# Three tiles of a depthwise convolution on TensorE with four taps stacked on partitions

## The chip, the core and the metric

The kernel runs on one core of a Trainium2 chip. The metric is the device time of one execution in microseconds; the time before is the median of three runs. A core has four engines that compute, each with an instruction stream of its own that it works through in order: TensorE (PE, matmuls), VectorE (DVE), ScalarE (ACT) and GpSimd (POOL). DMAs are issued from SP or from one of the other streams. What one engine needs of another it waits for on a semaphore.

## The reference

The program is two transformer blocks for 256 tokens of 1024 channels. The first block has two layers, each with a feed-forward part before and after its mixer; the mixer of the first layer is the convolution module that the change touches:

```python
def conv_module(h, w_pw1, w_dw, g_norm, w_pw2):
    u = h @ w_pw1
    a, b = jnp.split(u, 2, axis=-1)
    u = a * jax.nn.sigmoid(b)
    u = lax.conv_general_dilated(u, w_dw[:, None, :], window_strides=(1,),
        padding=[(CONV_WIDTH - 1, 0)], dimension_numbers=("NWC", "WIO", "NWC"),
        feature_group_count=D_MODEL)
    u = jax.nn.silu(rmsnorm(u, g_norm))
    return u @ w_pw2
```

CONV_WIDTH is 31, so every channel is its own causal filter of 31 taps over the tokens. Work of the second block that needs nothing of the first (the projections of its context tokens with `w_in_2`, gates, scans and states) is done early, beside the convolution.

## The kernel before

Channels lie on partitions: 1024 channels are 8 tiles of 128, tokens along the free axis. `conv` (L632) runs in about 210 to 385 us of the span. In a loop over four pairs of tiles it takes two parts of `conv_w_pw1`, projects (`proj_pair`), multiplies one half by the sigmoid of the other (L655 to L658) and leaves two tiles of `up`, 31 columns wider than the tokens. Weights come as 1 MB loads `raw` on SP; each part is split into a high piece `whi` on ScalarE (L193) and the rest `wlo` on VectorE (L197), and the projection takes three matmuls (L301 to L303) for each product.

The 31 taps of a tile are done in one of three ways:
- `taps` (L695) on VectorE: 31 instructions, the first L701, the others L703, each adding one shifted copy of `up` times a channel's weight into `cv`. Tiles 2, 3, 5, 6.
- `taps_pool` (L708): ScalarE makes four products at a time (L717, tile `taps`, two buffers), GpSimd sums them (L711). Tiles 0, 1, 4.
- `taps_pe` (L727) on TensorE: ScalarE scales the identity into 31 diagonal matrices (L736), TensorE adds 31 matmuls into one PSUM tile `ctaps` (L741, L744), ScalarE copies it out and squares it. Tile 7 (CONV_PE, at the end of the class).

These three are generators. `tick` (L353) takes pieces of the waiting ones while other code is written out: in the projections four pieces of VectorE's lane and one of GpSimd's per weight part (CONV_RATE = 4, 1), later sixteen and three per step (CONV_RATE2) of the loop that writes out the context's work (`fill` until "late"). That work is `cp` on TensorE in blocks of 16 matmuls (two records of the profile each; L1135, L1139), the sigmoids `sg` on ScalarE, gates `cfk` and scans on VectorE, the keys' norm (`ks`, `rsm` to `rx`, `krb`, `dup`), then transposes `ctr` and the state's matmuls `cs`. The order in which code is written out is the order of each engine's stream; nothing is moved afterwards.

At the end, `rstd_from_sum` takes the sums of squares of all tiles (`vsvector`, `vsgpsimd`), VectorE makes the scale (`rsm` to `dg`), TensorE broadcasts it (`rb`, L426), and the scaled result (L435) goes into the output projection `pd`.

Of the kernel before, what the change touches and what calls it, by code (L numbers as in the profile page):

```python
# [8 lines left out]
F32 = mybir.dt.float32  # L9
# [3 lines left out]
AF = mybir.ActivationFunctionType  # L13
ALU = mybir.AluOpType
# [3 lines left out]
P = 128  # L18
T = 256
D = 1024  # L20
KD = 8
# [20 lines left out]
def hmask(p):  # L42

    s, c = p[:, None] % 32, np.arange(32)[None, :]
    lv = []
    for b in (1, 2, 4, 8, 16):
        same = s // (2 * b) == c // (2 * b)
        lv.append(same & (s // b < c // b))
        lv.append(same & (s // b > c // b))
    return np.concatenate(lv, 1).astype(np.float32)  # L50


def constants():

    p = np.arange(P)
    f32 = np.float32
    parts = {}
    parts["ident"] = np.eye(P, dtype=f32)
    parts["ones"] = np.ones((P, P), f32)
    parts["iota_p"] = np.stack([p, p + P], 1).astype(f32)  # L60
    parts["other"] = (p[:, None] // 32 != np.arange(4)[None, :]).astype(f32) * 1024
    rot = np.zeros((P, P), f32)
    for m in range(P):
        b, r = divmod(m, 64)
        if r < 32:
            rot[b * 64 + r + 32, m] = -1.0
        else:
            rot[b * 64 + r - 32, m] = 1.0
    parts["rot"] = rot
    rot = np.zeros((P, P), f32)  # L70
    for m in range(P):
        b, r = divmod(m, 32)
        if r < 16:
            rot[b * 32 + r + 16, m] = -1.0
        else:
            rot[b * 32 + r - 16, m] = 1.0
    parts["rot_ax"] = rot
    for i in range(2):
        sel = np.zeros((P, P), f32)
        for m in range(P):  # L80
            sel[i * 64 + m % 64, m] = 1.0
        parts[f"dup{i}"] = sel
    parts["blk64"] = (p[:, None] // 64 == p[None, :] // 64).astype(f32)
    t = np.arange(T)
    ang = np.zeros((P, T), f32)
    for q in range(P):
        r = q % 64
        ang[q] = (t // 64 if r < 32 else t % 64).astype(f32) * INV_FREQ_AX[r % 16]
    parts["cos_ax"] = np.cos(ang.astype(np.float64)).astype(f32)
    parts["sin_ax"] = np.sin(ang.astype(np.float64)).astype(f32)  # L90
    parts["invf"] = INV_FREQ[p % 32][:, None]
    parts["hmask"] = hmask(p)
    parts["iota_t"] = np.broadcast_to(t.astype(f32), (P, T)).copy()
    cols, off = {}, 0
    for n, a in parts.items():
        cols[n] = (off, a.shape[1])
        off += a.shape[1]
    return np.ascontiguousarray(np.concatenate(list(parts.values()), 1)), cols


CONST, CCOL = constants()
N_IDENT = CCOL["rot"][0]
N_EARLY = CCOL["iota_t"][0]
# [158 lines left out]
def wcols(name, idx, c0, n, k0=0, nk=None):  # L262

    def load(A, eng, v):
        w = A[name]
        for i in idx:
            w = w[i]
        if len(w.shape) == 3:
            w = w.rearrange("c h d -> c (h d)")
        w = w.rearrange("(k p) f -> p k f", p=P)  # L270
        eng.dma_start(v, w[:, k0:k0 + nk, c0:c0 + n])
    return load
# [12 lines left out]
def two(a):  # L285

    return a.rearrange("p (a t) -> p a t", a=2)


class Kernel:  # L290
# [341 lines left out]
    def conv(self, x, sums, done, sp):  # L632
        nc = self.nc
        late = self.late_rb(sums)
        with self.tc.tile_pool(name="conv", bufs=1) as cp:
            up = cp.tile([P, KD, T + 32], F32, name="up")
            nc.gpsimd.memset(up[:, :, 0:32], 0.0)
            v = cp.tile([P, KD, T], F32, name="cv")

            self.vs = {n: cp.tile([P, T], F32, name="vs" + n) for n in ("vector", "gpsimd")}  # L640
            self.vs_used = []
            self.fillers += [self.context(cp, sp), self.adaln(1)]
            self.rate = self.CONV_RATE
            pe = []
            for c in range(4):
                w = self.S.get(KD, 256, wcols("conv_w_pw1", (0,), 1024 + 256 * c, 256, 0, KD))
                pb = self.proj_pair(w, x, KD)
                if c == 0:
                    next(late)
                w = self.S.get(KD, 256, wcols("conv_w_pw1", (0,), 256 * c, 256, 0, KD))  # L650
                pa = self.proj_pair(w, x, KD)
                if c == 0:
                    rb = next(late)
                sb = self.tmp.tile([P, 512], F32, name="sg", tag="sg")
                nc.vector.tensor_tensor(two(sb), two(pb), rb, op=ALU.mult)  # L655
                nc.scalar.activation(sb, sb, AF.Sigmoid)
                nc.vector.tensor_tensor(two(sb), two(sb), rb, op=ALU.mult)
                nc.vector.tensor_tensor(up[:, 2 * c:2 * c + 2, 32:], pa.rearrange("p (a t) -> p a t", a=2),  # L658
                                        sb.rearrange("p (a t) -> p a t", a=2), op=ALU.mult)
                for k in (2 * c, 2 * c + 1):  # L660
                    if k in self.CONV_PE:
                        pe.append(self.taps_pe(cp, v[:, k], up[:, k], k))
                    elif k in self.CONV_POOL:
                        self.background[1].append(self.taps_pool(cp, v[:, k], up[:, k], k))
                    else:
                        self.background[0].append(self.taps(v[:, k], up[:, k], k))
            pe = chain(*pe)
            while self.fill(1) != "late":
                self.tick(self.CONV_RATE2)
                next(pe, None)  # L670
            self.rate = 0, 0
            for _ in pe:
                pass
            self.tick_all()
            self.warm(AF.Sqrt)
            r = self.rstd_from_sum(self.tok_sums([self.vs[n] for n in self.vs_used]), D)
            w = self.S.ahead(2)
            dg = self.diag(r)
            self.fill(self.CONV_FILL[0])
            self.warm(AF.Silu)  # L680
            rb = self.bcast(r, dg)
            for low, eng in zip(w, (nc.vector, nc.gpsimd)):
                low(eng)
            self.S.n_hl = 2
            y = (sp.tile([P, KD, T], F32R, name="yh", tag="hc"), cp.tile([P, KD, T], F32R, name="yl", tag="cb"))
            b = cp.tile([P, 4, T], F32, name="taps", tag="taps", bufs=2)
            xn = cycle([b[:, i] for i in range(4)])
            self.apply_norm(v, rb, lambda k: self.V("conv_norm", k), y[0], y[1], KD, AF.Silu,
                            new=lambda: next(xn))
            self.fill(self.CONV_FILL[1])  # L690
            self.S.n_hl = self.N_HL
            return self.out_proj(y, KD, self.by_k("conv_w_pw2"), done(1.0, (self.CONV_FILL[2],) * 8),
                                 self.WIDE[0])
# [30 lines left out]
        self.add_sq_on("gpsimd", acc, pool.tile([P, 4, T], F32, name="taps", tag="taps", bufs=2)[:, 0])  # L724
        yield

    def taps_pe(self, pool, acc, u, k):  # L727

        nc = self.nc
        ps = self.psf.tile([P, 512], F32, name="ctaps", tag="f")  # L730
        todo = []
        for j0 in range(0, 32, 4):
            js = range(j0, min(j0 + 4, 31))
            dg = pool.tile([P, 4, P], F32, name="diag", tag="diag", bufs=2)
            for j in js:
                nc.scalar.activation(dg[:, j - j0], self.C("ident"), AF.Copy,  # L736
                                     scale=self.dw[:, j * KD + k:j * KD + k + 1])
            todo.append([(j, dg[:, j - j0]) for j in js])
            if j0:
                for j, d in todo.pop(0):  # L740
                    nc.tensor.matmul(ps[:, :T], d, u[:, 2 + j:2 + j + T], start=j == 0, stop=False)  # L741
            yield
        for j, d in todo.pop(0):
            nc.tensor.matmul(ps[:, :T], d, u[:, 2 + j:2 + j + T], start=False, stop=j == 30)  # L744
        nc.scalar.activation(acc, ps[:, :T], AF.Copy)
        self.vs_used.append("scalar")
        sq = pool.tile([P, 4, P], F32, name="diag", tag="diag", bufs=2)[:, 0:2].rearrange("p a b -> p (a b)")
        nc.scalar.activation(sq, ps[:, :T], AF.Square)
        self.vs["scalar"] = sq
        yield  # L750

    def add_sq_on(self, name, v, q):
# [1300 lines left out]
    MLA_FILL = 6, 1, 2, 0, 2, 4, 0  # L2053
    B2_FILL = 2, 4, 0
    B2_HL = 2
    CONV_PE = 7,
    CONV_POOL = (0, 1, 4)
    WIDE = (4, 2, 2), (2, 2, 2, 2), (4, 2, 2)
    CONV_RATE = 4, 1
# [43 lines left out]
```

## Time and profile before

| | before |
|---|---|
| median of 3 runs | 1808.44 us (1806.88 to 1810.2) |
| profiled execution | 1808.75 us |
| its span | 1807.0 us |
| mean granted TensorE clock | 0.94 |
| busy: TensorE, VectorE, ScalarE, GpSimd | 1604.6, 1001.2, 745.5, 314.8 us |

All times of rows are microseconds from the start of the span. A row of the timeline is one group of like instructions that follow each other on an engine: start, length, engine, line, operation, output and inputs, count, and in brackets the idle time ahead of it with the instruction that ended it. A q behind an engine's name marks its instruction stream, as for the issue of a DMA. Records of one matmul overlap, so the spacing of a run of matmuls is its length divided by its count. What ends last at a wait matters; the idle time of an engine that nobody waits for costs nothing.

### The profile page before, as it was taken

What the parts mean: (1) busy time and instruction counts of PE and PEld (TensorE: products, weight loads), DVE (VectorE), ACT (ScalarE), POOL (GpSimd) and SP (SyncE); (2) the same over time, 40 slices, a digit from 0 to 9 for tenths busy, and PEclk for the clock granted to TensorE, in tenths of its full rate; (3) what the DMA queues carried; (4) which work ended last, traced back from release to release, by engine and by line L of the source; (5) the groups of instructions that cost most, each with busy time, mean ns of one, the idle gap of its engine ahead of it and who ended that gap; (6) DMA issues with size and microseconds to landing.
All of it is one profiled execution on the core that took longest, in us unless ns stands there. A gap on an engine that the chain in (4) does not pass through costs nothing.

```text
span 1807.0 us, 29979 instructions
## 1 busy us (share of the span) xinstructions
PE 1604.6 (89%) x12517; PEld 1298.5 (72%) x12517; DVE 1001.2 (55%) x1638; ACT 745.5 (41%) x1254; POOL 314.8 (17%) x265
## 2 busy tenths in 40 slices
PE   8999998789999999999999999998988876766665
PEld 7887897688888888887988889877984432332322
DVE  6775689967765777664677646876651110101111
ACT  5654466456554655444665545545431000000001
POOL 1332157412220232010032120320010000000000
PEclk9999999899999999999999999999987988887987
DMA  7867642335556565566656557332789999999996
GB/s 214 282 226 253 221 140 94 117 93 188 187 172 201 169 207 182 166 204 224 212 186 189 178 192 237 114 95 71 297 334 360 419 418 419 419 419 419 419 419 281
DMA packets 239357, 435.29 MB, mean 241 GB/s; under 512 B 16514, under 2 KB 204596, under 8 KB 212596
## 3 DMA queue, kind: packets, MB, share of 16 engines
q1 hardware_dynamic: 238660, 431.52, 67.3%
q8 instruction: 98, 1.61, 0.4%
q0 software_dynamic: 528, 1.84, 0.3%
q14 instruction: 39, 0.32, 0.1%
q10 hardware_dynamic: 32, 0.01, 0.0%
HBM read 432.29 MB, written 1.05 MB: 240 GB/s over the span
## 4 chain that ended last, share of the span: by engine, by line
PE 61%; DMA 19%; DVE 13%; ACT 3%; issue 2%; POOL 1%; SPq 0%; DVEq 0%; ACTq 0%; POOLq 0%
PE mm L308 16%; DMA raw<-in_w_exp_up_dram 11%; PE pd L308 9%; PE mm L310 8%; DMA raw<-in_w_exp_down_dram 7%; PE pd L310 5%; DVE cv L703 4%; PE mm L301 3%; PE mm L303 3%; PE mm L302 3%; DVE wlo L197 3%; PE gu L1787 3%; PE dn L1819 1%; PE pd L302 1%; PE pd L301 1%
## 5 line engine op out<-in xcount | busy, mean ns | idle before, releaser
L197 DVE TENSOR_TENSOR wlo<-raw,whi 128x1024 fp32r<-128x1024 f32 (+1 forms) x381 | 487.6, 1305 | 169.9 <-ACT whi L193 169.6
L308 PE MATMUL mm<-x,whi 128*128 128x512 f32 x1376 | 478.8, 396 | 0.6 <-ACT whi L193 0.5
L193 ACT ACTIVATE whi<-raw 128x1024 fp32r<-128x1024 f32 (+1 forms) x381 | 381.0, 1028 | 151.5 <-PE pd L308 73.9
L310 PE MATMUL mm<-x,wlo 128*128 128x256 f32 x1376 | 372.1, 281 | 1.5 <-DVE wlo L197 1.5
L308 PEld LDWEIGHTS mm<-x,whi 128*128 128x128 f32 x1376 | 253.2, 188 | 55.3 <-ACT whi L193 1.1
L310 PEld LDWEIGHTS mm<-x,wlo 128*128 128x128 f32 x1376 | 259.8, 189 | 9.3 <-DVE wlo L197 2.3
L308 PE MATMUL pd<-hh,whi 128*128 128x512 f32 x704 | 247.0, 397 | 1.9 <-DVE hc L1119 1.8
L1787 PE MATMUL gu<-raw,xe 128*32 128x256 f32 x2048 | 159.1, 449 | 58.1 <-DMA raw<-in_w_exp_up_dram 31.5
L310 PE MATMUL pd<-hh,wlo 128*128 128x256 f32 x704 | 193.0, 282 | 0.8 <-DVE wlo L197 0.8
L1787 PEld LDWEIGHTS gu<-raw,xe 128*32 128x32 f32 x2048 | 63.3, 123 | 134.4 <-DMA raw<-in_w_exp_up_dram 48.9
L308 PEld LDWEIGHTS pd<-hh,whi 128*128 128x128 f32 x704 | 131.1, 189 | 33.0 <-issue 2.8
L303 PE MATMUL mm<-x,wlo 128*128 128x256 f32 (+1 forms) x512 | 148.1, 289 | 5.8 <-DVE wlo L197 5.8
L301 PE MATMUL mm<-x,whi 128*128 128x256 f32 (+1 forms) x512 | 150.3, 294 | 3.1 <-ACT whi L193 2.6
L302 PE MATMUL mm<-x,whi 128*128 128x256 f32 (+1 forms) x512 | 147.8, 289 | 0.3 <-DVE x L440 0.3
L310 PEld LDWEIGHTS pd<-hh,wlo 128*128 128x128 f32 x704 | 133.6, 190 | 4.0 <-DVE wlo L197 1.4
L1801 DVE TENSOR_TENSOR mhd<-gu,msg 128x256 f32<-128x256 f32 x16 | 9.6, 602 | 225.9 <-ACT msg L1796 225.9
L607 POOL TENSOR_TENSOR sg<-sg,rbs 128x512 f32<-128x512 f32 x43 | 68.4, 1591 | 257.9 <-DVE sg L538 230.9
L1819 PE MATMUL dn<-raw,mht 128*32 128x256 f32 x1024 | 82.9, 474 | 32.3 <-DMA raw<-in_w_exp_down_dram 18.9
L301 PEld LDWEIGHTS mm<-x,whi 128*128 128x128 f32 (+1 forms) x512 | 100.8, 197 | 8.0 <-ACT whi L193 3.2
L303 PEld LDWEIGHTS mm<-x,wlo 128*128 128x128 f32 (+1 forms) x512 | 100.7, 197 | 6.6 <-DVE wlo L197 6.6
L302 PEld LDWEIGHTS mm<-x,whi 128*128 128x128 f32 (+1 forms) x512 | 100.8, 197 | 0.6 <-DVE x L440 0.5
L486 POOL TENSOR_TENSOR ssum<-ssum,sq 128x256 f32<-128x256 f32 x48 | 37.6, 788 | 364.6 <-ACT sq L485 364.3
(458 smaller groups left out, 2322.9 us busy)
## 6 DMA issues: line engine op xcount, KB each, us to landing
raw<-in_ffn_w_dram SPq DMA_DIRECT2D x120, 1024.0 KB
raw<-in_w_exp_gate_dram SPq DMA_DIRECT2D x64, 1024.0 KB
raw<-in_w_exp_up_dram SPq DMA_DIRECT2D x64, 1024.0 KB
raw<-in_w_exp_down_dram SPq DMA_DIRECT2D x64, 1024.0 KB
raw<-in_w_in_dram SPq DMA_DIRECT2D x28, 1024.0 KB
raw<-in_w_mod_dram SPq DMA_DIRECT2D x24, 1024.0 KB
raw<-in_ffn_w_dram SPq DMA_DIRECT2D x16, 768.0 KB
raw<-in_conv_w_pw_dram SPq DMA_DIRECT2D x12, 1024.0 KB
```

Source lines behind the costliest of these rows:

```text
L193: nc.scalar.activation(hi, r, AF.Copy)
L197: eng.tensor_tensor(lo, r, hi.bitcast(F32), op=ALU.subtract)
L301: mm(ps, w[0], x[0], start=start, stop=False, **kw)
L302: mm(ps, w[0], x[1], start=False, stop=False, **kw)
L303: mm(ps, w[1], x[0], start=False, stop=stop, **kw)
L308: both = lambda: mm(ps, w[0], x[2][:, k].rearrange("p a t -> p (a t)"), start=start, stop=stop, skip_group_check=True)
L310: low = lambda: mm(ps[:, :T], w[1], x[0][:, k], start=False, stop=False, skip_group_check=True)
L486: (eng or nc.vector).tensor_tensor(ssum, ssum, s, op=ALU.add)
L607: eng.tensor_tensor(two(sg), pg, rb, op=ALU.mult)
L703: self.nc.vector.scalar_tensor_tensor(acc, src, g, acc, op0=ALU.mult, op1=ALU.add)
L1787: nc.tensor.matmul(pg[32 * j:32 * j + 32, m * T:(m + 1) * T], xe[:, 2 * c + i, slots], w[:, i, 256 * j:256 * j + 256], start=c == 0 and m ...
L1819: nc.tensor.matmul(pd[32 * g:32 * g + 32, :T], ht[:, i, 32 * j:32 * j + 32], w[:, i, 256 * g:256 * g + 256], start=j == 0 and i == 0, stop ...
```

## The change

CONV_PE becomes 3, 5, 6; tile 7 goes to VectorE's `taps`, so that VectorE keeps tiles 2 and 7. `taps_pe` computes in another way. A tile's 128 channels are four groups g of 32. A copy `u4` (name `u_2409`, `u_2599`, `u_2882` for tiles 3, 5, 6 in the rows below) holds, for each group, the 32 channels four times on the 128 partitions, the copy a shifted by a tokens: 16 DMAs issued on ScalarE's queue, 32 partitions x 284 columns, 36 KB each. A matrix W4 of 32 columns for each group and each of eight steps r holds the weights of the taps 4r to 4r + 3; VectorE makes it with two 128x512 products of a constant (`ident4`) and `dw4`, into the two buffers of the state S0 (`state_83`, `state_84`). 32 matmuls (128 rows, 32 columns, 256 tokens) then give the tile, four column groups side by side. ScalarE copies the result out; VectorE squares and adds it.

`dw4` is filled at the start of `conv` by a memset on GpSimd and 16 small copies on VectorE. `up` is four columns wider, with a memset of its own. The copies of tiles 3 and 5 are issued right behind their `up`, those of tile 6 in the first step of the context loop; the matrix of tile 3 right behind its copies; the other steps are spread over the context loop: tile 3's matmuls and tile 6's copies, tile 5's matrix, its matmuls, tile 6's matrix, its matmuls.

```diff
             for c in range(4):
...
                 for k in (2 * c, 2 * c + 1):
                     if k in self.CONV_PE:
-                        pe.append(self.taps_pe(cp, v[:, k], up[:, k], k))
+                        pe.append(self.taps_pe(*((cp, "u4"), (sp, "xs"))[len(pe) % 2], v[:, k], up[:, k], k))
+                        for _ in range(max(0, 3 - len(pe))):
+                            next(pe[-1])
...
-            pe = chain(*pe)
+            steps = iter(((0, 2), (1,), (1,), (2,), (2,)))
             while self.fill(1) != "late":
                 self.tick(self.CONV_RATE2)
-                next(pe, None)
+                for i in next(steps, ()):
+                    next(pe[i])
...
-    def taps_pe(self, pool, acc, u, k):
+    def taps_pe(self, pool, tag, acc, u, k):
         nc = self.nc
+        u4 = pool.tile([P, 4, T + 28], F32, name="u4", tag=tag)
+        for a in range(4):
+            for g in range(4):
+                nc.scalar.dma_start(u4[32 * a:32 * a + 32, g], u[32 * g:32 * g + 32, 2 + a:T + 30 + a])
+        yield
+        w4 = [st.rearrange("p h v -> p (h v)").rearrange("p (a c) -> p a c", c=32) for st in self.S0]
+        for i in range(2):
+            nc.vector.tensor_tensor(w4[i], self.C("ident4").unsqueeze(1).to_broadcast([P, 16, 32]),
+                                    self.dw4[:, k, 2 * i:2 * i + 2].rearrange("p g r -> p (g r)").unsqueeze(2)
+                                    .to_broadcast([P, 16, 32]), op=ALU.mult)
+        yield
         ps = self.psf.tile([P, 512], F32, name="ctaps", tag="f")
...
+        for r in range(8):
+            for g in range(4):
+                nc.tensor.matmul(ps[32 * g:32 * g + 32, :T], w4[g // 2][:, 8 * (g % 2) + r], u4[:, g, 4 * r:4 * r + T],
+                                 start=r == 0, stop=r == 7)
         nc.scalar.activation(acc, ps[:, :T], AF.Copy)
...
+        self.add_sq_on("vector", acc, self.tmp.tile([P, T], F32, name="xn", tag="xn"))
         yield
...
-    CONV_PE = 7,
+    CONV_PE = 3, 5, 6
```

ScalarE's stream of before, from the sigmoid of pair 2 on:

```order
L656 ACTIVATE sg<-sg 128x512
L193 ACTIVATE whi<-raw 128x1024
L717 ACTIVATE taps<-up,dw 128x256 x16
L656 ACTIVATE sg<-sg 128x512
L1179 ACTIVATE cak<-cp 128x256
L1075 ACTIVATE sq<-cak 128x256
L1184 ACTIVATE vall<-cp 128x256
L717 ACTIVATE taps<-up,dw 128x256 x11
L736 ACTIVATE diag<-cst,dw 128x128 x4
L1191 ACTIVATE cV<-cp 128x2x256
```

The same place of ScalarE's stream in the changed kernel:

```order
L667 ACTIVATE sg<-sg 128x512
L747 DMA u_2599<-up 32x284 x16
L194 ACTIVATE whi<-raw 128x1024
L730 ACTIVATE taps<-up,dw 128x256 x16
L667 ACTIVATE sg<-sg 128x512
L1192 ACTIVATE cak<-cp 128x256
L1088 ACTIVATE sq<-cak 128x256
L1197 ACTIVATE vall<-cp 128x256
L730 ACTIVATE taps<-up,dw 128x256 x11
L761 ACTIVATE cv<-ctaps 128x256
L747 DMA u_2882<-up 32x284 x16
L1204 ACTIVATE cV<-cp 128x2x256
```

The 16 copies of tile 5 stand between the sigmoid and the split of the next weight part, where nothing stood; those of tile 3 stand likewise one pair earlier, and those of tile 6 ahead of `cV`. Behind this `cV` the stream goes on with the `rss` of the keys, 3 products `taps`, another `cV` and 12 products.

VectorE's stream of before, from the end of the keys' norm on (`cfk` is the context's gate; 16 taps stand between the `up` of pair 3 and this norm):

```order
L1061 COPY rx<-rsr 128x128 x2
L703 SCALAR_TENSOR_TENSOR cv<-up,dw,cv 128x256 x14
L757 TENSOR_TENSOR vsvector<-cv 128x256
L759 TENSOR_TENSOR xn<-cv 128x256
L760 TENSOR_TENSOR vsvector<-vsvector,xn 128x256
L701 TENSOR_SCALAR cv<-up,dw 128x256 x2
L703 SCALAR_TENSOR_TENSOR cv<-up,dw,cv 128x256 x14
L1051 TENSOR_SCALAR cfk<-sg,lb 128x256 x2
```

The same place in the changed kernel (between the `up` of pair 3 and the norm stand the first 16 taps of tile 7 and the square of tile 3):

```order
L1074 COPY rx<-rsr 128x128 x2
L716 SCALAR_TENSOR_TENSOR cv<-up,dw,cv 128x256 x15
L772 TENSOR_TENSOR xn<-cv 128x256
L773 TENSOR_TENSOR vsvector<-vsvector,xn 128x256
L752 TENSOR_TENSOR state_83<-mid,dw_2088 128x512
L752 TENSOR_TENSOR state_84<-mid,dw_2088 128x512
L772 TENSOR_TENSOR xn<-cv 128x256
L773 TENSOR_TENSOR vsvector<-vsvector,xn 128x256
L1064 TENSOR_SCALAR cfk<-sg,lb 128x256 x2
```

The 15 taps here are the last of tile 7, the only tile on VectorE here,, and the two products at L752 that make tile 5's matrix stand behind all of them.

TensorE's stream of before, behind the projections (`cp` is the context):

```order
L1139 MATMUL cp<-raw,hc 128x256 x16
L1081 MATMUL ks<-mid,sq 128x2 x2
L741 MATMUL ctaps<-up,diag 128x256 x4
L1139 MATMUL cp<-raw,hc 128x256 x16
L741 MATMUL ctaps<-up,diag 128x256 x4
L1135 MATMUL cp<-hc,raw 128x256 x16
```

And in the changed kernel, from the block ahead of `ks` on, with the first two of the sixteen rows of tile 5:

```order
L1152 MATMUL cp<-raw,hc 128x256 x16
L1094 MATMUL ks<-mid,sq 128x2 x2
L1152 MATMUL cp<-raw,hc 128x256 x16
L759 MATMUL ctaps<-u_2599,state_83 32x256 x2
L759 MATMUL ctaps<-u_2599,state_84 32x256 x2
```

All 32 matmuls of a tile stand in one piece now: tile 3's ahead of the first of these blocks, tile 5's behind the second, tile 6's behind the fourth.

## Rows read from the trace of the kernel before

**Rows 1.** Busy time by stretch; columns: stretch, length, each engine's busy time.

```profile
210.00:235.00 25.00, 25.00 (x188) 23.82 (x187) 14.17 (x24) 13.66 (x19) 1.73 (x3) 1.00 0.65 205
260.00:290.00 30.00, 25.83 (x153) 24.18 (x153) 28.29 (x34) 11.02 (x27) 18.00 (x18) 0.89 0.34 106
345.00:364.00 19.00, 6.74 (x27) 5.34 (x25) 18.90 (x42) 6.34 (x16) 0.04 (x1) 0.73 0.35 111
```

**Rows 2.** Waits, 225 to 386 us: engine, waited for: sum, times, longest.

```profile
POOL taps L711 <- ACT taps L717: 37.2, 7, 13.9
...
PE ctr L1160 <- DVE cfk L1151: 11.3, 1, 11.3
```

**Rows 3.** Timeline of DMA issues on SP and ScalarE, and of ScalarE.

```profile
26.97 0.55 SPq L1850 DMA_DIRECT2D state<-in_q_norm_g_dram  x2
...
0.76 0.42 ACTq L1969 DMA_DIRECT2D state<-in_ffn_norm_dram  x1
...
247.53 1.04 ACT L193 ACTIVATE whi<-raw 128x1024 fp32r<-128x1024 f32 x1
248.47 1.70 ACT L717 ACTIVATE taps<-up,dw 128x256 f32<-128x256 f32 x4
```

**Rows 4.** Timeline of VectorE, pairs 1 to 3 of the convolution.

```profile
248.45 0.69 DVE L658 TENSOR_TENSOR up<-mm,sg 128x512 f32<-128x512 f32 x1
249.06 1.53 DVE L197 TENSOR_TENSOR wlo<-raw,whi 128x1024 fp32r<-128x1024 f32 x1
...
271.26 0.69 DVE L658 TENSOR_TENSOR up<-mm,sg 128x512 f32<-128x512 f32 x1
271.87 1.22 DVE L197 TENSOR_TENSOR wlo<-raw,whi 128x1024 fp32r<-128x1024 f32 x1
273.00 14.30 DVE L703 SCALAR_TENSOR_TENSOR cv<-up,dw,cv 128x256 f32<-128x256 f32 x16
...
289.39 0.69 DVE L658 TENSOR_TENSOR up<-mm,sg 128x512 f32<-128x512 f32 x1
290.00 11.71 DVE L703 SCALAR_TENSOR_TENSOR cv<-up,dw,cv 128x256 f32<-128x256 f32 x16
```

**Rows 5.** Timeline of VectorE behind the projections.

```profile
301.64 0.15 DVE L382 TENSOR_SCALAR rsm<-ks 128x4 f32<-128x4 f32 x1
...
303.34 12.71 DVE L703 SCALAR_TENSOR_TENSOR cv<-up,dw,cv 128x256 f32<-128x256 f32 x14
...
331.87 6.41 DVE L703 SCALAR_TENSOR_TENSOR cv<-up,dw,cv 128x256 f32<-128x256 f32 x16
...
366.44 0.73 DVE L1051 TENSOR_SCALAR cfk<-sg,lb 128x256 f32<-128x256 f32 x2
```

**Rows 6.** Timeline of TensorE behind the projections.

```profile
299.55 7.07 PE L1139 MATMUL cp<-raw,hc 128*128 128x256 f32 x32
306.46 1.89 PE L741 MATMUL ctaps<-up,diag 128*128 128x256 f32 x8
...
315.09 0.38 PE L1070 MATMUL krb<-cst,rx 128*128 128x128 f32 x2
...
332.58 1.03 PE L1089 MATMUL dup<-cak,mid 128*128 128x256 f32 x4
...
373.17 1.06 PE L426 MATMUL rb<-dg,cst 128*128 128x128 f32 x4
```

**Rows 7.** Groups by line and shape: busy, mean ns of one, idle before (the sigmoids 225 to 386 us).

```profile
L1787 PE MATMUL gu<-raw,xe 128*32 128x256 f32 x2048 | 159.1, 449 | 58.1 <-DMA raw<-in_w_exp_up_dram 31.5 <-DMA raw<-in_w_exp_gate_dram 26.6
...
L1047 ACT ACTIVATE sg<-cp 128x512 f32<-128x512 f32 x8 | 4.5, 596 | 17.5 <-DVE cfk L1051 16.6 <-DVE cfk L1054 0.9
```

**Rows 8.** Timeline of GpSimd beside the taps of 331.87 us.

```profile
333.87 5.54 POOL L711 TENSOR_TENSOR taps<-taps 128x512 f32<-128x512 f32 x1 [6.54 <-ACT taps L717]
```

**Rows 9.** DMA issues by tile: engine, count, KB each, median us to landing.

```profile
spare<-in_final_norm_g_dram POOLq DMA_DIRECT2D x1, 512.0 KB, 8.1
posi<-in_positions_dram POOLq DMA_DIRECT2D x1, 128.0 KB, 3.8
```

## The prediction before the run

> **What bounds the kernel now.** I read the busy table by stretch first. In 260 to 290 us VectorE is busy 28.29 of 30 us, and in 345 to 364 us 18.90 of 19, while TensorE works 6.74 of those 19 [rows 1]. The waits say who waits: TensorE's longest of the conv stretch, 11.3 us, is `ctr` for VectorE's `cfk`, and GpSimd waits 37.2 us in seven pieces for ScalarE's products `taps` [rows 2]. So the end of the conv, `rb` at 373.17 us [rows 6], hangs on VectorE, whose taps of tiles 2, 3, 5, 6 stand between its pieces of context work. Behind `rb` everything shifts as a whole: what `rb` gains or loses, the kernel does. The profiled execution took 1808.75 us with a span of 1807.0; the sum is made against 1808.75, 0.3 above the median of 1808.44.
>
> **The change part by part.**
>
> *Removed and swapped.* VectorE drops the 93 taps of tiles 3, 5, 6 and takes the 31 of tile 7: 62 fewer. At 0.40 us (16 in 6.41 [rows 5]) to 0.89 us (16 in 14.30 [rows 4]) that is 25 to 55 us of its time. ScalarE loses the diagonals of tile 7, TensorE the 31 full matmuls. If VectorE's busy time were all that counts, this would be a clear gain; the order in which the new pieces stand decides how much is left.
>
> *The copies.* Each of three tiles is copied by 16 DMAs of 36 KB issued on ScalarE, whose stream is in order. The only DMA that ScalarE issues in this trace took 0.42 us; two small ones on SP took 0.55 together, 0.275 each [rows 3]. I take ScalarE's own price: 16 x 0.42 = 6.7 us a group, with 4.4 as the low end. The Trainium skill ("DMA: Bandwidth & Descriptors", section "Anatomy of one DMA — SWDGE (gpsimd) path") puts the sequencer's dispatch at about 50 ns and most of a DMA's fixed cost behind it, in the receipt of the data; by that a group would hold ScalarE for an estimated 0.8 us. The two rows disagree with that figure as a price of issue, by five times and more.
>
> *First group, tile 3.* It needs `up` of pair 1, done at 248.45 + 0.69 = 249.1 [rows 4], so it runs to 255.9. Behind it stands `whi`, which ran at 247.53 to 248.6 before `up` was ready [rows 3]; now it ends at 256.9. VectorE's `wlo` needs it: before it took 249.06 to 250.6 [rows 4], now 1.53 us from 256.9 to 258.4. That is 7.8 later, and the next pieces (four taps a weight part, as before) follow at the same spacing, so `up` of pair 2 ends at 272.0 + 7.8 = 279.8. The two products that build the tap matrix of tile 3 (128x512, 0.69 each by the `up` rows) fall in VectorE's wait.
>
> *Second group, tile 5.* 279.8 + 6.7 = 286.5, then `whi` 1.04, then `wlo` 1.22: 288.8 in place of 271.87 + 1.22 = 273.1 [rows 3, 4]. 15.7 late in all. Behind it stand 15 taps of tile 2 and a square where there were 16 taps: no difference. `up` of pair 3 was done at 290.1 [rows 4], now 305.8.
>
> *VectorE up to the second tap matrix.* Tiles 5 and 6 are finished on TensorE, but the tap matrix of tile 5, W4(5), stands on VectorE behind all of tile 7: 16 taps 11.7 (as at 290.00 [rows 4]), square and add 1.4, the `rsm` chain 303.34 - 301.64 = 1.7, 15 taps 13.6 (12.71 for 14 [rows 5]), square and add 1.4, the matrix 1.4. In sum 31.2, so it is ready at 337.0. The taps take these long prices where GpSimd works beside them: 16 cost 6.41 while GpSimd waited or was itself held (one of its sums took 5.54 there [rows 5, 8]), 11.7 to 14.3 otherwise. I take the long ones, because ScalarE's list feeds GpSimd 16, 11, 3 and 12 products in just these stretches.
>
> *TensorE from there.* Its matmuls stand in a fixed order: tile 3, two blocks of context, tile 5, two blocks, tile 6, two blocks. It is ready for tile 5 by about 322 us (the projection over some 3 us behind the `wlo` of 288.8, then 24 smaller `cp` matmuls, at most 10.6 by the blocks' price, tile 3 in 5.0, two blocks in 14.1), so it waits for W4(5). From 337.0: tile 5 takes 32 matmuls of 32 columns, 64 records; 2048 records of that shape in four column groups took 159.1 us, 0.078 each [rows 7], so 5.0; a block of 32 records takes 7.07, `krb` 0.4, `dup` 1.0 [rows 6]. 2 x 5.0 + 4 x 7.07 + 1.4 = 39.7, so the last block ends at 376.7. If the column groups did not overlap here, the 8 records of `ctaps` in 1.89 [rows 6] give 0.22 to 0.24 each, 14 a tile and 18 more on the path.
>
> *The tail.* After the last block come two sigmoids (0.6 each [rows 7]) and what ran from `cfk` at 366.44 to `rb` at 373.17 [rows 5, 6], 6.7. `rb` comes at 376.7 + 1.2 + 6.7 = 384.6, 11.4 later than before. The squares of tiles 5 and 6 lie before that on VectorE, which by then has little else.
>
> *Edits at nothing.* The third group (tile 6) stands on ScalarE beside TensorE's wait for W4(5); with that wait gone, 4.4 to 6.7 come back, and ScalarE's `cV` and the products for GpSimd behind it are late. The 16 small copies that fill dw4 cost about 0.15 each (nearest `rsm`, 0.15 [rows 5]), 2.4 us; VectorE is busy 14.17 of 25 us there [rows 1] and has room, but TensorE is busy all 25, so up to 2.4 shows if they delay the scale of the first pair. GpSimd's memsets lie where it is busy 1.73 of 25. The 32 more constant columns go with an early load.
>
> *Sum.* 1808.75 + 11.4 = about 1820.
>
> **The rivals.**
>
> *A, the issues are cheap: no change that can be measured.* If an issue held ScalarE for nothing, `whi` would still wait for `up`, as it stands behind the copies: the two `wlo` are late by 1.1 and 2.3, W4(5) is ready at 323.6 and `rb` at 371.2: 1807. With SP's 4.4 a group the delays are 5.5 and 11.1, W4(5) at 332.4, `rb` at 380.0: 1815. For it: SP's small issues at 0.275; against: ScalarE's own row. Break-even is W4(5) at 325.6. By the Trainium skill's figure of the section above an estimated 1808 would come out.
>
> *B, the taps get cheap: faster.* While the copies hold ScalarE, GpSimd gets no products (it waited 37.2 us for them before [rows 2]) and does not hold VectorE. The 15 + 16 + 15 taps on my path cost 13.4 + 11.7 + 13.6 = 38.7; at 6.41 for 16 they cost 18.4. All of that gives 1820 - 20 = 1800; from 11.4 of those 20.3 on the change is faster. For it: VectorE has 62 taps less. Against: after each group of copies ScalarE goes straight to GpSimd's products. With 4.4 a group as well, 1795.
>
> *C, slower still.* The ninth to sixteenth copy of a group wait for the landing of an earlier one. A landing of 3.8 us is the shortest shown for another queue, 8.1 the longest [rows 9]; the ninth is due 3.4 after the first. At 8.1 a group costs 4.7 more, two of them 9: 1829. Without overlap of the column groups, 18 more: 1838.
>
> **How the numbers follow.** The forecast case (1812 to 1826) gets 0.50, A 0.15, B 0.23, C 0.12. The likeliest time is 1820. B spans 1795 to 1805, half of it below 1800; about half of C lies above 1830; so 1800 to 1830 leaves out not quite 2 in 10. A measurement of this kernel tells about 0.2%, 3.6 us, from no change. Faster than that is nearly all of B with the low end of A, 0.24; within it, 1805 to 1812, most of A and the edge of the forecast, 0.18; slower 0.58.
>
> **What will show it.** Right: ScalarE's issues run 6 to 7 us a group with `whi` right behind; `wlo` after pair 1 starts near 257, `up` of pair 3 ends near 306, TensorE's longest wait of the stretch is tile 5's matmuls for the product on VectorE, ending near 337, and `rb` is near 385. A: a group in under 2 us. B: tile 7's taps under 0.6 us each. C: gaps between the issues, or over 0.15 us a record in tile 3's matmuls. The forecast is wrong from the start if `whi` does not wait for the copies.

## The result and the profile after

| | before | changed |
|---|---|---|
| median | 1807.66 us (4 runs) | 1827.78 us (4 runs, 1822.48 to 1830.91) |
| ratio | | 1.0114, 95% interval 1.0096 to 1.0132 |
| span of the profiled execution | 1807.0 us | 1829.1 us |
| `rb`, the end of the convolution | 373.17 us | 396.17 us |
| busy: VectorE, ScalarE | 1001.2, 745.5 us | 981.2, 736.3 us |

The change costs 20.1 us. VectorE and ScalarE are both less busy than before, and `rb` still comes 23.0 us later: the kernel lost by waiting, not by working. The loss lies between 250 and 350 us, and three views show it.

ScalarE's timeline of the changed kernel (start, length, engine, line, operation, tiles, count, idle time before with what ended it; ACTq is its instruction stream):

```profile
250.31 10.23 ACTq L747 DMA_DIRECT2D u<-up  x16
260.58 1.06 ACT L194 ACTIVATE whi<-raw 128x1024 fp32r<-128x1024 f32 x1 [11.82 <-DMA u<-up]
...
283.89 10.33 ACTq L747 DMA_DIRECT2D u<-up  x16
294.27 1.06 ACT L194 ACTIVATE whi<-raw 128x1024 fp32r<-128x1024 f32 x1 [11.93 <-DMA u<-up]
...
319.65 10.18 ACTq L747 DMA_DIRECT2D u<-up  x14
329.87 0.60 ACT L1204 ACTIVATE cV<-cp 128x512 f32<-128x512 f32 x1 [9.91 <-DMA u<-up]
...
331.78 0.21 ACT L394 ACTIVATE rss<-rsm 128x4 f32<-128x4 f32 x1
```

Three groups of 16 copies, each over 10 us long (the first two copies of the third, at 318.45 and 319.01, stand on lines of their own). Behind the first two waits the split of a weight part, which before ran at once [rows 3]; behind the third wait the context's `cV` and the keys' `rss`. The view of that one line of code gives the length of a single issue, least, median and most in ns:

```profile
L747 ACTq DMA_DIRECT2D u<-up x48: 514/601/612, 250.3 to 329.3; - x48
```

VectorE's timeline, the places that answer to [rows 4, 5]:

```profile
222.87 3.53 DVE L647 COPY dw<-dw 32x64 f32<-32x64 f32 x16 [1.26 <-POOL dw L642]
...
249.59 0.69 DVE L669 TENSOR_TENSOR up<-mm,sg 128x512 f32<-128x512 f32 x1
...
261.67 1.22 DVE L198 TENSOR_TENSOR wlo<-raw,whi 128x1024 fp32r<-128x1024 f32 x1 [9.35 <-ACT whi L194]
...
283.17 0.69 DVE L669 TENSOR_TENSOR up<-mm,sg 128x512 f32<-128x512 f32 x1
295.36 1.23 DVE L198 TENSOR_TENSOR wlo<-raw,whi 128x1024 fp32r<-128x1024 f32 x1 [11.49 <-ACT whi L194]
296.50 14.31 DVE L716 SCALAR_TENSOR_TENSOR cv<-up,dw,cv 128x256 f32<-128x256 f32 x15
...
313.37 0.69 DVE L669 TENSOR_TENSOR up<-mm,sg 128x512 f32<-128x512 f32 x1
...
314.48 11.97 DVE L716 SCALAR_TENSOR_TENSOR cv<-up,dw,cv 128x256 f32<-128x256 f32 x15
...
332.02 0.18 DVE L395 RECIPROCAL rsr<-rss 128x4 f32<-128x4 f32 x1 [4.70 <-ACT rss L394]
...
333.30 14.10 DVE L716 SCALAR_TENSOR_TENSOR cv<-up,dw,cv 128x256 f32<-128x256 f32 x15
...
348.24 1.28 DVE L752 TENSOR_TENSOR state<-mid,dw 128x512 f32<-128x512 f32 x2
```

The reader sees the delays add up: `up` of pair 1 is 1.1 us late, that of pair 2 11.9, that of pair 3 24.0; then VectorE waits 4.70 us for the `rss` that ScalarE's third group holds; and only behind tile 7's last 15 taps comes the matrix of tile 5, ready at 349.5. In the kernel before, the wait for the `rss` was 0.27 us:

```profile
302.06 0.18 DVE L394 RECIPROCAL rsr<-rss 128x4 f32<-128x4 f32 x1 [0.27 <-ACT rss L393]
```

The 1.1 us at pair 1 understate what the filling of `dw4` costs. The last `h` ahead of the convolution, whose code the change leaves alone, came 1.7 us earlier in this profile than in that of the kernel before (first line before, second changed):

```profile
221.80 0.42 DVE L504 SCALAR_TENSOR_TENSOR h<-pd,h 128x256 f32<-128x256 f32 x1
220.13 0.42 DVE L505 SCALAR_TENSOR_TENSOR h<-pd,h 128x256 f32<-128x256 f32 x1
```

From this `h` to `up` of pair 0 the changed kernel took 16.5 us (236.66 less 220.13) where 13.7 sufficed before (235.52 less 221.80), so `dw4` is worth 2.8. Where this `h` stands is scatter: in the eleven profiles of the changed kernel and its edits it comes between 219.1 and 222.5. The stretch behind `rb` scatters as well, from 1428.6 to 1435.1 us in all twelve profiles, so `rb` tells the time to about 3 us.

TensorE's timeline, which answers to [rows 6]:

```profile
307.89 3.66 PE L759 MATMUL ctaps<-u,state 128*32 128x256 f32 x64
...
349.02 6.63 PE L759 MATMUL ctaps<-u,state 128*32 128x256 f32 x64 [23.02 <-issue]
...
369.82 3.66 PE L759 MATMUL ctaps<-u,state 128*32 128x256 f32 x64
...
381.28 7.07 PE L1148 MATMUL cp<-hc,raw 128*128 128x256 f32 x32
...
396.17 1.22 PE L427 MATMUL rb<-dg,cst 128*128 128x128 f32 x4 [0.33 <-DVE dg L418]
```

TensorE stands still for 23.02 us ahead of tile 5. The profile puts it down to "issue", that is, it shows no releaser; the matmuls start 0.8 us behind the start of VectorE's two products, when the first of them is done, and e2 below shows that they wait for these.

### The profile page after: what moved, and what is told of

The parts are those of the page before. It is cut to its first block, busy times and chain, and to the rows that moved or that the text cites. A ratio compares the mean times of both kernels' runs of the same rounds, so it can differ in the third digit from the quotient of the medians.

```text
span 1829.1 us, 30233 instructions
## 1 busy us (share of the span) xinstructions
PE 1606.1 (88%) x12643; PEld 1298.4 (71%) x12643; DVE 981.2 (54%) x1600; ACT 736.3 (40%) x1224; POOL 311.5 (17%) x267
## 4 chain that ended last, share of the span: by engine, by line
PE 58%; DMA 22%; DVE 10%; ACT 4%; issue 3%; ACTq 1%; POOL 1%; DVEq 0%; SPq 0%; POOLq 0%
PE mm L309 16%; DMA raw<-in_w_exp_up_dram 13%; PE pd L309 9%; PE mm L311 8%; DMA raw<-in_w_exp_down_dram 8%; PE pd L311 4%; DVE wlo L198 3%; PE mm L302 3%; PE mm L304 3%; PE mm L303 3%; DVE cv L716 2%; ACTq L747 1%; PE gu L1800 1%; PE pd L303 1%; PE pd L302 1%
```

## The experiments

Each is an edit of the changed kernel. Its ratio is to the kernel before on the same chip.

**e1, the copies issued on SP.**

```diff
-                nc.scalar.dma_start(u4[32 * a:32 * a + 32, g], u[32 * g:32 * g + 32, 2 + a:T + 30 + a])
+                nc.sync.dma_start(u4[32 * a:32 * a + 32, g], u[32 * g:32 * g + 32, 2 + a:T + 30 + a])
```

> The changed kernel with the 48 copies of u4 issued on SP in place of ScalarE; nothing else. Theory 1 (the issues themselves, 16 x 0.64 = 10.3 us a group, hold ScalarE's stream, and with it the split of the next weight part): the two waits of 11.8 us of the split are gone, up of pair 3 ends near 293 (314 in the changed kernel, 290 before), the matrix of tile 5 is ready near 324 (349.5), rb near 371 (396.2), and the time is 1800 to 1806. Theory 2 (it is the landing of the copies, or a semaphore, that is waited for, whoever issues them): the split still starts 10 us late and the time stays at 1825 to 1830. Theory 3 (the copies then stand ahead of the weight loads on SP, 10 us a group): the raw loads come late, TensorE waits for them, 1810 to 1825.

Measured: 1805.28 us, ratio 1.0003 (0.9987 to 1.0019). The whole loss of the change is gone. SP's timeline, then TensorE's:

```profile
250.18 10.55 SPq L747 DMA_DIRECT2D u<-up  x16
275.04 10.48 SPq L747 DMA_DIRECT2D u<-up  x16
...
```

```profile
324.05 6.36 PE L759 MATMUL ctaps<-u,state 128*32 128x256 f32 x64 [19.88 <-issue]
...
370.95 1.22 PE L427 MATMUL rb<-dg,cst 128*128 128x128 f32 x4
```

A group takes as long on SP as on ScalarE, 10.5 us, but there nothing urgent stands behind it: theory 1, within half a microsecond at tile 5's start (324 forecast) and at `rb` (371). Theories 2 and 3 fall. The wait ahead of tile 5 is still there, 19.9 us; e3 tries what it is worth. The Trainium skill ("DMA: Bandwidth & Descriptors", section "Rules for kernel authors") says that spreading DMAs over several issuing engines gives no bandwidth and saves only sequencer issue time. These two kernels bear on the issue time alone: it was moved rather than saved, and off ScalarE it was worth 20 us on the path; no run here tests the bandwidth.

**e2, tile 5's matrix one step earlier** (behind 16 of tile 7's taps instead of 31), the copies still on ScalarE.

```diff
-            steps = iter(((0, 2), (1,), (1,), (2,), (2,)))
+            steps = iter(((0, 2, 1), (), (1,), (2,), (2,)))
```

> The changed kernel with the tap matrix of tile 5 built one step earlier, behind the first 16 taps of tile 7 and not behind all 31; the copies stay on ScalarE. Theory 1 (TensorE's wait of 23.0 us is for this matrix, and the order on VectorE sets it): the matrix is ready near 328.5, TensorE starts tile 5 there, rb near 376, the time is 1805 to 1811. Rival (something else is just behind: the products for GpSimd, or the keys' norm held by the third group of copies): under half of the 20 us come back, 1817 to 1826.

Measured: 1820.16 us, ratio 1.0087 (1.0069 to 1.0105). TensorE's timeline:

```profile
328.78 4.27 PE L759 MATMUL ctaps<-u,state 128*32 128x256 f32 x64 [1.71 <-issue]
...
357.27 6.61 PE L759 MATMUL ctaps<-u,state 128*32 128x256 f32 x64 [9.99 <-ACT sg L1060]
...
386.00 0.74 PE L427 MATMUL rb<-dg,cst 128*128 128x128 f32 x4 [0.46 <-DVE dg L418]
```

Tile 5 starts 20.2 us earlier, at 328.8 as forecast: the wait was for this matrix. But `rb` gains only 10.2, half of it, and the rival's time comes out: a wait of the same kind opens ahead of tile 6. The profile names ScalarE's sigmoid for it; that is the last of several, and the one that lasts is VectorE's:

```profile
333.51 15.07 DVE L716 SCALAR_TENSOR_TENSOR cv<-up,dw,cv 128x256 f32<-128x256 f32 x15
...
356.49 1.28 DVE L752 TENSOR_TENSOR state<-mid,dw 128x512 f32<-128x512 f32 x2
```

Tile 6's matrix stands behind the same 15 taps, two squares with their sums and the first gates, and TensorE starts when its first half is done. Of the rival's own causes the keys' norm shows as 2.88 us, VectorE's wait for the `rss` ahead of these taps.

**e3, both edits.**

> Both edits: copies on SP, matrix of tile 5 one step earlier. If the two costs lie one behind the other on the path, they add up: up of pair 3 near 293, the matrix near 306, rb near 354, 1783 to 1790, which is faster than the kernel before. If the end is then set by GpSimd's tiles (their last sum came at 345 us before) or by VectorE's taps of tile 7, rb stays above 362 and the time is 1793 to 1800. If SP's loads suffer, above that.

Measured: 1795.04 us, ratio 0.995 (0.9934 to 0.9966), faster than the kernel before. TensorE's timeline:

```profile
306.69 6.73 PE L759 MATMUL ctaps<-u,state 128*32 128x256 f32 x64 [3.23 <-issue]
...
332.05 0.72 PE L759 MATMUL ctaps<-u,state 128*32 128x256 f32 x4 [4.41 <-ACT sg L1060]
...
360.45 1.22 PE L427 MATMUL rb<-dg,cst 128*128 128x128 f32 x4 [0.46 <-DVE dg L418]
```

The two costs lie one behind the other: 0.0111 for the queue and 0.0027 for the order taken alone make 0.0138, both together 0.0164. The time itself lies in the range of the other branch, 1793 to 1800, though `rb` came ahead of that branch's 362. `rb` came 6 us later than the 354 of the expectation. Tile 5's matrix was in time: TensorE waits 3.2 us for it and starts at 306.7. What the expectation lacked is tile 6: TensorE waits 4.8 us (4.41 and 0.37) for its matrix, and its matmuls behind that wait took 5.9 us in place of 3.7. That the two costs add up is as much as the intervals allow: 0.0138 and 0.0164 are not told apart.

**e4, the 16 copies into dw4 moved** from the start of the convolution to behind `up` of pair 0.

> The changed kernel with the 16 copies into dw4 moved from the start of the convolution to behind up of pair 0. In the changed kernel they took 3.53 us on VectorE ahead of two wlo. If they cost the path about 2.8 us there and nothing where they now stand, the time is 1823 to 1826; if they only move to ahead of the wlo of pair 1 and are paid there, it stays at 1826 to 1829.

Measured: 1827.92 us, ratio 1.0121 (1.0100 to 1.0142), no gain shown. VectorE's timeline:

```profile
233.84 6.73 DVE L670 COPY dw<-dw 32x64 f32<-32x64 f32 x16
240.60 6.80 DVE L198 TENSOR_TENSOR wlo<-raw,whi 128x1024 fp32r<-128x1024 f32 x4
```

The cost only moved. From the last `h` to `up` of pair 0 it is 13.7 us again, as before the change, but from there to `up` of pair 1 16.8 in place of 12.9. At the start the copies took 3.53 us; here, beside GpSimd's first sums, 6.73, and four `wlo` come out in a row behind them.

**e5, both matrices earlier, copies on SP.** Tile 5's is built behind `up` of pair 3 in two scratch buffers (the two of the state still hold tile 3's there), tile 6's where e3 built tile 5's.

```diff
-            steps = iter(((0, 2), (1,), (1,), (2,), (2,)))
+            next(pe[1])
+            steps = iter(((0, 2, 2), (), (1,), (), (2,)))
...
-                nc.scalar.dma_start(u4[32 * a:32 * a + 32, g], u[32 * g:32 * g + 32, 2 + a:T + 30 + a])
+                nc.sync.dma_start(u4[32 * a:32 * a + 32, g], u[32 * g:32 * g + 32, 2 + a:T + 30 + a])
...
+        if k == 5:
+            w4 = [self.tmp.tile([P, 512], F32, name="hd", tag="hd").rearrange("p (a c) -> p a c", c=32) for i in range(2)]
```

> Copies on SP, and the tap matrices earlier still: that of tile 5 right behind up of pair 3, in two scratch buffers of its own (free until the transposes), that of tile 6 where tile 5's was in e3, behind the first 16 taps of tile 7. In e3 TensorE waited 3.2 us for the first and 4.8 for the second. Theory 1 (TensorE's order now sets the end, so each such wait counts in full): both waits gone, rb near 351 (360.5 in e3), 1784 to 1789. Rival (VectorE's second 15 taps of tile 7 with four squares and the gates, or GpSimd's last sum near 340, end just behind): rb stays above 357, 1791 to 1796.

Measured: 1789.64 us, ratio 0.9896 (0.9867 to 0.9925), the fastest of all. TensorE's timeline:

```profile
305.21 3.66 PE L762 MATMUL ctaps<-u,hd 128*32 128x256 f32 x64
...
323.04 3.66 PE L762 MATMUL ctaps<-u,state 128*32 128x256 f32 x64
...
348.28 1.94 PE L1176 MATMUL ctr<-cst,cfk 128*128 128x128 f32 x8 [6.63 <-DVE cfk L1167]
...
357.06 0.94 PE L427 MATMUL rb<-dg,cst 128*128 128x128 f32 x4
```

Both waits for a matrix are gone, as theory 1 has it, and the tiles take 3.66 us each. But `rb` came at 357.1, at the rival's bound, and the time lies in neither range: TensorE now waits 6.63 us for VectorE's `cfk`, the wait that was 11.3 in the kernel before [rows 2]. So VectorE does end just behind, as the rival has it; GpSimd's last sum, at 344.1, is no part of that wait.

**e6, each copy cut in two.** The same bytes, 32 issues a group, on ScalarE.

```diff
-                nc.scalar.dma_start(u4[32 * a:32 * a + 32, g], u[32 * g:32 * g + 32, 2 + a:T + 30 + a])
+                for o in (0, 142):
+                    nc.scalar.dma_start(u4[32 * a:32 * a + 32, g, o:o + 142],
+                                        u[32 * g:32 * g + 32, 2 + a + o:2 + a + o + 142])
```

> The changed kernel with each copy cut into two of half the width, 32 issues a group on ScalarE, the same bytes. Theory 1 (an issue has a fixed price of 0.64 us, whatever its size): a group takes 20.5 us, the first two delay up of pair 3 by 20.5 more, and the third delays the keys' norm by 10 more: 1848 to 1860. Rival (ScalarE is held by the bytes or by the landing): a group stays near 10 us and the time at 1825 to 1832.

Measured: 1859.32 us, ratio 1.0296 (1.0271 to 1.0321). ScalarE's timeline, then VectorE's:

```profile
251.28 20.48 ACTq L748 DMA_DIRECT2D u<-up  x32
...
295.10 20.40 ACTq L748 DMA_DIRECT2D u<-up  x32
```

```profile
364.14 0.18 DVE L395 RECIPROCAL rsr<-rss 128x4 f32<-128x4 f32 x1 [15.53 <-ACT rss L394]
```

Half the columns, the same 0.64 us each: the price does not go by the bytes. Each half still has its 32 rows, so a price for each row of a copy is not told apart from one for each issue. The wait for the `rss` grew by the 10.8 that the third group grew by.

**e7 and its repetition e10, only the third group on SP.** e9 is the changed kernel once more, beside e10.

```diff
-                nc.scalar.dma_start(u4[32 * a:32 * a + 32, g], u[32 * g:32 * g + 32, 2 + a:T + 30 + a])
+                (nc.sync if k == 6 else nc.scalar).dma_start(u4[32 * a:32 * a + 32, g], u[32 * g:32 * g + 32, 2 + a:T + 30 + a])
```

> The changed kernel with only the third group of copies, tile 6's, issued on SP. The prediction had this group hidden behind TensorE's wait. Theory 1 (it is not: it holds the rss of the keys' norm on ScalarE, for which VectorE waited 4.7 us with tile 7's last 15 taps and tile 5's matrix queued behind): the wait is gone, the matrix is ready 4 to 5 us earlier, 1821 to 1824. Rival (hidden): 1825 to 1830.

> The changed kernel itself once more, beside the next one on the same chip, since two comparisons with the kernel before did not tell the third group's part: 1.0114 as before, and the time 4 to 5 us above the next kernel's if the keys' norm is held by that group, level with it if not.

> Only tile 6's copies on SP, once more beside the changed kernel: 4 to 5 us below it (ratio near 1.009) if what the trace of e7_third_sp shows at rb, 4.6 us earlier, reaches the end; level with it if something behind rb gives it back.

Measured: e7 1826.36 us, ratio 1.0114 (1.0094 to 1.0134); e9 1828.77, 1.0117 (1.0101 to 1.0134); e10 1825.19, 1.0105 (1.0091 to 1.0120). VectorE's and TensorE's timelines of e7:

```profile
327.85 0.18 DVE L395 RECIPROCAL rsr<-rss 128x4 f32<-128x4 f32 x1 [0.27 <-ACT rss L394]
```

```profile
344.86 6.22 PE L759 MATMUL ctaps<-u,state 128*32 128x256 f32 x64 [17.89 <-issue]
...
391.59 1.22 PE L427 MATMUL rb<-dg,cst 128*128 128x128 f32 x4
```

The wait for the `rss`, 4.70 us in the changed kernel and 5.03 in e9's trace, is 0.27 in the traces of e7 and e10. In e7's, tile 5 starts 4.2 us earlier and `rb` comes 4.6 earlier. The times agree in sign, 1.4 us between the changed kernel and e7 and 3.6 between e9 and e10, but their intervals overlap and e7's ratio is that of the changed kernel, so that it reaches the end is likely, not shown.

**e8, the copies of tiles 3 and 5 issued late,** behind `up` of pair 3, on ScalarE, with tile 3's matrix.

```diff
-                        for _ in range(max(0, 3 - len(pe))):
-                            next(pe[-1])
...
+            for i in (0, 0, 1):
+                next(pe[i])
             steps = iter(((0, 2), (1,), (1,), (2,), (2,)))
```

> The changed kernel with the copies of tiles 3 and 5, and tile 3's matrix, issued behind up of pair 3 and not behind their own; all on ScalarE as before. No split of a weight part stands behind them now. If the splits held were all the loss: up of pair 3 near 291, the time 1803 to 1808. Theory 1 with ScalarE's whole stream in view: 32 issues hold it from 292 to 312, then the 11 products, tile 3's copy-out near 319 and the third group stand where they stood, the rss comes near 330 as before, tile 5's matrix near 349: 1822 to 1830.

Measured: 1825.27 us, ratio 1.0105 (1.0082 to 1.0127): no gain clear of the noise, though no split waits for copies any more. ScalarE's, VectorE's and TensorE's timelines:

```profile
289.58 20.51 ACTq L747 DMA_DIRECT2D u<-up  x32
310.14 0.38 ACT L1192 ACTIVATE cak<-cp 128x256 f32<-128x256 f32 x1 [19.93 <-DMA u<-up]
```

```profile
293.23 7.78 DVE L716 SCALAR_TENSOR_TENSOR cv<-up,dw,cv 128x256 f32<-128x256 f32 x15
317.43 0.67 DVE L772 TENSOR_TENSOR xn<-cv 128x256 f32<-128x256 f32 x1 [16.43 <-ACT cv L761]
...
328.23 0.18 DVE L395 RECIPROCAL rsr<-rss 128x4 f32<-128x4 f32 x1 [9.19 <-ACT rss L394]
```

```profile
345.24 6.89 PE L759 MATMUL ctaps<-u,state 128*32 128x256 f32 x64 [24.90 <-issue]
...
392.66 1.22 PE L427 MATMUL rb<-dg,cst 128*128 128x128 f32 x4 [0.46 <-DVE dg L418]
```

The 30 us of issues stay on ScalarE's stream. Instead of the splits they hold the copy-out of tile 3 (VectorE waits 16.43 us for it) and the `rss` (9.19), and tile 5 starts 3.8 us earlier than in the changed kernel. So it is not the early start of the copies that costs, but on whose stream they are.

## Why the prediction was right in its way and short in its size

The forecast was 1820, in 1800 to 1830, slower; measured 1827.78. Measured against the medians the loss is 20.1 us where 11.4 was forecast. The path was the right one: the queue, the splits, tile 5's matrix, TensorE's wait for it. But the time lies above the 1812 to 1826 of the forecast case and inside the range only by the room made for C, whose mechanisms did not come; that much is luck. By its steps:

- *The copies hold ScalarE and the splits behind them.* Right (e1). The term was mis-sized: 6.7 us a group, taken from the one DMA that ScalarE issued before [rows 3], with 4.4 as a low end and no end above. It measured 10.2 to 10.3: 0.60 an issue and a start every 0.64. `up` of pair 3 came 24.0 us late in place of 15.7, and 25.7 counted from the last `h` ahead of the convolution. Of the 10.0 more, 2.8 are dw4's and the other 7.2 the two groups'.
- *dw4 at nothing, at the most 2.4.* The copies took 3.5 us and a wait of 1.3 for GpSimd's memset; `up` of pair 0 came 2.8 later, counted from that `h`. In the place that e4 tried they were no cheaper; no other was tried.
- *The third group hidden beside TensorE's wait.* Wrong. It does lie beside that wait, but it also holds the `rss`, on which VectorE's chain to the end of that very wait hangs: 4.4 us more of chain (6.1 for the 1.7 taken), shown in the traces of e7 and e10.
- *Tile 5's matrix behind all of tile 7.* Right: it was forecast for 337.0 and ready at 349.5, 35.5 us behind `up` of pair 3 in place of 31.2, and the difference is the `rss`. TensorE waited 23.0 us. What the prediction did not say is that tile 6's matrix has the same fault one step later (e2).
- *From the matrix to `rb`:* 47.6 forecast, 46.7 measured. The tile behind the long wait took 6.63 in place of 5.0, the next one 3.66.
- Summed: 11.4 + 2.8 (dw4) + 7.2 (groups) + 4.3 (`rss`) - 0.9 (the rest) = 24.8; less the 1.7 by which the convolution began earlier in this profile, 23.1, and `rb` moved by 23.0.

The rivals: A fell, an issue costs more, not less. B fell: ScalarE goes straight from the copies to GpSimd's products, and 15 taps cost 14.31, 11.97 and 14.10. Its mechanism is real all the same: in e8, with ScalarE held and GpSimd without products, 15 taps cost 7.78. Of C neither mechanism came: the issues follow each other without gaps, so no landing is waited for, and a record of the 32-column matmuls took 0.057 us (3.66 for 64).

The Trainium skill gives its 50 ns for the sequencer's dispatch ("DMA: Bandwidth & Descriptors", section "Anatomy of one DMA — SWDGE (gpsimd) path") for DMAs issued from GpSimd. The prediction carried it over to ScalarE, and there it is no price of an issue: the median of 48 is 601 ns on ScalarE and 589 ns on SP (e1). The skill's rule to coalesce transfers under 64 KB (section "Rules for kernel authors") the runs bear out: cut from 36 KB to 18 KB, the copies cost ScalarE twice the time.

## What to carry to other kernels

A DMA is work for the engine that issues it: count the issues, price them by their own kind and with an end above the nearest row, and put them on a stream where nothing urgent stands behind. When work moves from a busy engine to an idle one, look at what the busy engine still has to prepare for it and where that stands in its order; here two small products, last in line, kept TensorE waiting for 23 us. Each wait that is removed shows the next: queue, first matrix, second matrix, then VectorE again.

## What the runs showed of the hardware

- An issue of a copy of 32 partitions by 284 columns from SBUF to SBUF took 0.60 us on ScalarE and 0.59 on SP (e1), and with 142 columns it held ScalarE as long (20.48 for 32 issues); earlier rows show 0.275 and 0.42 for other transfers [rows 3]. What makes the difference was not tried.
- 32-column matmuls in four column groups: 64 records in 3.66 us, 0.057 each, where a record of the full-width `ctaps` of before took 0.24 (8 in 1.89 [rows 6]). Right behind the idle 23 us they took 6.63. The table by stretch of the changed kernel (stretch, length, busy time of PE, PEld, DVE, ACT, POOL, then the granted clock) shows most of why:

```profile
349.00:355.60 6.60, 6.58 (x65) 5.66 (x65) 0.53 (x1) 0.00 (x0) 0.00 (x0) 0.59 0.00 0
369.80:373.40 3.60, 3.60 (x65) 1.98 (x64) 2.13 (x3) 3.41 (x9) 3.36 (x5) 1.00 0.66 214
```

  Behind the idle time the granted clock is 0.59 of full speed on average: 0.50, the 1.2 GHz level, up to 354 us, and 0.85 from there to 355.6. The tile after it has 1.00, the 2.4 GHz level. In e5, where nothing is waited for ahead of tile 5, it takes 3.66 us at 1.00. Part of what the wait costs is paid behind it: 3.0 us.
- Copies of 32 partitions by 64 elements on VectorE took 0.22 us each alone and 0.42 beside GpSimd (e4).
